# A gated product over 8192 rows: each group's store split into even and odd partitions on two queues, and the second half worked in three pieces

## The chip, the cores and the metric

The kernel runs on one core of one Trainium2 chip. The metric is device time in microseconds of one execution; the time before is the median of three runs. The profile is one more execution, recorded by the hardware profiler.

## The reference

```python
x = np.random.randn(8192, 8192).astype(np.float32)      # fixed seed

def reference(x):
    a, b = np.split(x, 2, axis=-1)        # each 8192 x 4096
    silu_b = b / (1 + np.exp(-b))
    return a * silu_b                     # 8192 x 4096, float32
```

Each element of the input is read once, 268.44 MB, and each element of the output is written once, 134.22 MB.

## The kernel before

The rows are taken four at a time: one partition holds four rows of the input, 128 KB, in two halves of 64 KB. A group is 128 partitions, so 512 rows, and there are 16 groups. There are three tiles of 128 x 16384 float32 (64 KB in a partition): `pack0` and `pack1`, which take the first half (two rows) of even and odd groups, and `extra`, which takes the second half of every group. The gate is worked in place; the products of both halves are written into the group's `pack`, which then is the complete output of the four rows and is stored from there.

```python
R = 4
W = R * half                                   # 16384
xv = x.tensor.reshape([N // R, R * M]).ap()    # 2048 x 32768
ov = out.tensor.reshape([N // R, W]).ap()      # 2048 x 16384
G = N // (P * R)                               # 16 groups
last = G - 1
packs = [pool.tile([P, W], x.dtype, name=f"pack{s}") for s in range(2)]
extra = pool.tile([P, W], x.dtype, name="extra")
# ... ordered(inst, *after): inst waits only for what is named in after
def load(eng, g, h, *after):
    tile_ = extra if h else packs[g % 2]
    return ordered(
        eng.dma_start(out=tile_, in_=xv[g * P : (g + 1) * P, h * W : (h + 1) * W]), *after
    )

def swiglu(g, h, k0, k1, *after, behind=()):
    rows = (extra if h else packs[g % 2]).rearrange("p (k s c) -> p k s c", k=2, s=2)
    o = packs[g % 2].rearrange("p (h k c) -> p h k c", h=2, k=2)
    b = rows[:, k0:k1, 1, :]
    gate = ordered(nc.scalar.activation(out=b, in_=b, func=_SILU), *after)        # L63
    return ordered(
        nc.vector.tensor_mul(out=o[:, h, k0:k1, :], in0=rows[:, k0:k1, 0, :], in1=b),  # L65
        gate, *behind,
    )

def store(eng, g, c0, c1, *after):
    return ordered(
        eng.dma_start(out=ov[g * P : (g + 1) * P, c0:c1], in_=packs[g % 2][:, c0:c1]), *after
    )

first = {0: load(nc.sync, 0, 0)}
second = {0: load(nc.sync, 0, 1)}
first[1] = load(nc.sync, 1, 0)
for g in range(G):
    prod = swiglu(g, 0, 0, 2, first[g])
    prod = swiglu(g, 1, 0, 1, second[g], behind=[prod])
    prod = swiglu(g, 1, 1, 2, behind=[prod])
    if g < last:
        second[g + 1] = load(nc.sync, g + 1, 1, prod)
    stored = store(nc.sync if g >= last - 1 else nc.scalar, g, 0, W, prod)
    if g + 2 < G:
        first[g + 2] = load(nc.sync, g + 2, 0, stored)
```

So the next load of `extra` waits for the last product of the group, which reads it, and the load of the group after next into the same `pack` waits until the store out of it has landed. The stores of the first 14 groups are issued on ScalarE's queue, those of the last two on SP's, on which all loads are.

Of the kernel before, what the change touches and what calls it, by code (L numbers as in the profile page):

```python
# [1 line left out]

# [4 lines left out]

_SILU = mybir.ActivationFunctionType.Silu


@with_exitstack
def kernel(
    ctx: ExitStack,
    tc: tile.TileContext,
    x: bass.AP,
    out: bass.AP,
):

    nc = tc.nc
    N, M = x.shape
    half = M // 2
    P = nc.NUM_PARTITIONS
    R = 4
    W = R * half

    xv = x.tensor.reshape([N // R, R * M]).ap()
    ov = out.tensor.reshape([N // R, W]).ap()
    G = N // (P * R)
    last = G - 1

    pool = ctx.enter_context(tc.tile_pool(name="sbuf", bufs=1))
    ctx.enter_context(tc.manual_schedule())
    packs = [pool.tile([P, W], x.dtype, name=f"pack{s}") for s in range(2)]
    extra = pool.tile([P, W], x.dtype, name="extra")

    ops = []

    def ordered(inst, *after):

        before = [t for t in reversed(ops) if t.ins.engine == inst.ins.engine][:1]
        for t in ops:
            if not any(t is k for k in [*after, *before]):
                tc.declare_no_dep(inst.ins, t.ins, reason="ordered by the other waits")
        ops.append(inst)
        return inst  # L50
# [4 lines that stand above are left out]
            eng.dma_start(out=tile_, in_=xv[g * P : (g + 1) * P, h * W : (h + 1) * W]), *after  # L55
        )

    def swiglu(g, h, k0, k1, *after, behind=()):

        rows = (extra if h else packs[g % 2]).rearrange("p (k s c) -> p k s c", k=2, s=2)  # L60
        o = packs[g % 2].rearrange("p (h k c) -> p h k c", h=2, k=2)
        b = rows[:, k0:k1, 1, :]
        gate = ordered(nc.scalar.activation(out=b, in_=b, func=_SILU), *after)  # L63
        return ordered(
            nc.vector.tensor_mul(out=o[:, h, k0:k1, :], in0=rows[:, k0:k1, 0, :], in1=b),  # L65
            gate, *behind,
        )

    def store(eng, g, c0, c1, *after):
        return ordered(  # L70
            eng.dma_start(out=ov[g * P : (g + 1) * P, c0:c1], in_=packs[g % 2][:, c0:c1]), *after
        )

    first = {0: load(nc.sync, 0, 0)}
    second = {0: load(nc.sync, 0, 1)}
    first[1] = load(nc.sync, 1, 0)
    for g in range(G):
        prod = swiglu(g, 0, 0, 2, first[g])
        prod = swiglu(g, 1, 0, 1, second[g], behind=[prod])
        prod = swiglu(g, 1, 1, 2, behind=[prod])  # L80
        if g < last:
            second[g + 1] = load(nc.sync, g + 1, 1, prod)
        stored = store(nc.sync if g >= last - 1 else nc.scalar, g, 0, W, prod)
        if g + 2 < G:
            first[g + 2] = load(nc.sync, g + 2, 0, stored)


# [1 line left out]
_INS = ['x']  # L89
_OUTS = [((8192, 4096), 'float32')]  # L90


# [23 lines left out]
```

## Time and profile before

| what | value |
| --- | --- |
| time, median of 3 | 967.15 us (965.48 to 969.77) |
| span of the profiled execution | 964.3 us |
| bytes read, written | 268.44 MB, 134.22 MB |
| queue 1 (SP): packets, MB | 4896, 285.21 |
| queue 10 (ScalarE): packets, MB | 2016, 117.44 |
| gate of 128 x 8192, of 128 x 4096 | 7029 ns, 3608 ns |
| product of 128 x 8192, of 128 x 4096 | 8692 ns, 4421 ns |
| issue to landing, median: load of pack, load of extra, store | 29.7, 47.2, 44.2 us |

How to read it: the busy row of the profile cuts the span into 40 equal slices and gives each a digit, the busy share in tenths. The DMA row is the mean over the core's 16 DMA engines. The chain is the work that ended last, followed back from the end; a DMA in it is counted from its issue to its landing, time in the queue included. In the table of stretches the columns are the stretch, its length, the busy time (and instructions) of VectorE, ScalarE and GpSimd, the granted TensorE clock, the DMA share and the GB/s. DVE is VectorE, ACT is ScalarE, POOL is GpSimd, and a name with q behind it is that engine's queue of DMA-issuing instructions.

### The profile page before, as it was taken

The page shows a single profiled execution, that of the slowest core. Times are in us where ns is not written, and L with a number is a line of the kernel's source. Part 1 is how long each engine was busy: PE and PEld are TensorE (multiplying, and loading weights), DVE is VectorE, ACT ScalarE, POOL GpSimd, SP SyncE. Part 2 cuts the span into 40 slices and gives each one's busy share as a digit, 9 for nine tenths or more (in the row PEclk, how much of TensorE's full clock was granted, in tenths as well). Part 3 has the DMA queues.
Part 4 walks back from the last instruction along what each step waited for, and adds up shares of the span by engine and source line. Part 5 has one row for each costly group of instructions (what it writes and reads, how often), then busy time and mean ns, then how long its engine had stood idle before and what let it go on. Part 6 is the DMA issues. An engine that isn't in the chain of part 4 may idle for free.

```text
span 964.3 us, 220 instructions
## 1 busy us (share of the span) xinstructions
DVE 279.2 (29%) x48; ACT 227.7 (24%) x49; POOL 0.2 (0%) x4
## 2 busy tenths in 40 slices
DVE  0423332133321333213332033321333213332250
ACT  1420222202222022220222112222022220222220
POOL 0000000000000000000000000000000000000000
DMA  9999999999999999999999999999999999999998
GB/s 400 427 435 435 413 430 421 421 432 397 435 427 402 435 394 435 424 402 435 413 435 413 391 435 400 435 427 391 435 410 430 410 405 435 392 435 416 432 410 351
DMA packets 6914, 402.67 MB, mean 418 GB/s; under 512 B 768, under 2 KB 768, under 8 KB 768
## 3 DMA queue, kind: packets, MB, share of 16 engines
q1 hardware_dynamic: 4896, 285.21, 71.0%
q10 hardware_dynamic: 2016, 117.44, 28.1%
q14 instruction: 2, 0.02, 0.0%
HBM read 268.44 MB, written 134.22 MB: 418 GB/s over the span
## 4 chain that ended last, share of the span: by engine, by line
DMA 76%; DVE 14%; ACT 6%; DVEq 0%; issue 0%; SPq 0%
DMA extra<-in_x_dram 76%; DVE pack L65 14%; ACT extra L63 6%; DVEq L111 0%; SPq L55 0%
## 5 line engine op out<-in xcount | busy, mean ns | idle before, releaser
L65 DVE TENSOR_TENSOR pack<-pack 128x8192 f32<-128x8192 f32 x16 | 139.1, 8692 | 340.8 <-ACT pack L63 340.8
L65 DVE TENSOR_TENSOR pack<-extra 128x4096 f32<-128x4096 f32 x32 | 140.2, 4421 | 317.2 <-ACT extra L63 317.2
L63 ACT ACTIVATE extra<-extra 128x4096 f32<-128x4096 f32 x32 | 114.0, 3608 | 398.4 <-DMA extra<-in_x_dram 398.4
L63 ACT ACTIVATE pack<-pack 128x8192 f32<-128x8192 f32 x16 | 112.5, 7029 | 305.1 <-DMA pack<-in_x_dram 305.1
L63 ACT ACT_TABLE_LOAD x1 | 1.3, 1283 | 0.7 <-PEq L100 0.7
L100 POOL MEMSET const-bfloat16-1.0<- 128x1 bf16 x1 | 0.1, 101 | 0.0
L100 POOL MEMSET const-uint8-127<- 128x1 uint8 x1 | 0.1, 101 | 0.0
L100 POOL MEMSET const-float32-0.0<- 128x1 f32 x1 | 0.1, 98 | 0.2 <-issue 0.2
L100 POOL MEMSET const-float32-1.0<- 128x1 f32 x1 | 0.1, 98 | 0.0
## 6 DMA issues: line engine op xcount, KB each, us to landing
pack<-in_x_dram SPq DMA_DIRECT2D x16, 29.7
extra<-in_x_dram SPq DMA_DIRECT2D x16, 47.2
out_dram<-pack ACTq DMA_DIRECT2D x14, 44.2
out_dram<-pack SPq DMA_DIRECT2D x2, 37.6
```

The source lines that it names most:

```text
L63: gate = ordered(nc.scalar.activation(out=b, in_=b, func=_SILU), *after)
L65: nc.vector.tensor_mul(out=o[:, h, k0:k1, :], in0=rows[:, k0:k1, 0, :], in1=b),
L100: nc = _bacc.Bacc("TRN2", target_bir_lowering=False, num_devices=1)
```

## The change

Three things are done. The store of each of the first 14 groups becomes two: the 64 even partitions on ScalarE's queue and the 64 odd ones on GpSimd's, so that both can be at work at once; the next load into the `pack` waits for both. The gates and products of the second half are done in three pieces (half a row, half a row, a row) in place of two, so that the first product can start earlier. The last two stores stay whole on SP's queue. The diff, cut to its core:

```diff
-    def swiglu(g, h, k0, k1, *after, behind=()):
-        ... gate of rows k0 to k1, then their product
+    def gate(g, h, k0, k1, c0, c1, *after):
+        b = rows(g, h)[:, k0:k1, 1, c0:c1]
+        return ordered(nc.scalar.activation(out=b, in_=b, func=_SILU), *after)
+    def product(g, h, k0, k1, c0, c1, *after):
+        ... the product of the same columns
-    def store(eng, g, c0, c1, *after):
+    def store(eng, g, parts, *after):
         return ordered(
-            eng.dma_start(out=ov[g * P : (g + 1) * P, c0:c1], in_=packs[g % 2][:, c0:c1]), *after
+            eng.dma_start(out=ov[g * P : (g + 1) * P][parts], in_=packs[g % 2][parts]), *after
         )
+    even, odd, whole = slice(0, P, 2), slice(1, P, 2), slice(0, P)
     ...
     for g in range(G):
-        prod = swiglu(g, 0, 0, 2, first[g])
-        prod = swiglu(g, 1, 0, 1, second[g], behind=[prod])
-        prod = swiglu(g, 1, 1, 2, behind=[prod])
+        prod = product(g, 0, 0, 2, 0, half, gate(g, 0, 0, 2, 0, half, first[g]))
+        pieces = [(0, 0, half // 2), (0, half // 2, half), (1, 0, half)]
+        gated = [gate(g, 1, k, k + 1, c0, c1, second[g]) for k, c0, c1 in pieces]
+        for (k, c0, c1), b in zip(pieces, gated):
+            prod = product(g, 1, k, k + 1, c0, c1, b, prod)
         if g < last:
             second[g + 1] = load(nc.sync, g + 1, 1, prod)
-        stored = store(nc.sync if g >= last - 1 else nc.scalar, g, 0, W, prod)
+        if g < last - 1:
+            stored = [store(nc.scalar, g, even, prod), store(nc.gpsimd, g, odd, prod)]
+        else:
+            stored = [store(nc.sync, g, whole, prod)]
         if g + 2 < G:
-            first[g + 2] = load(nc.sync, g + 2, 0, stored)
+            first[g + 2] = load(nc.sync, g + 2, 0, *stored)
```

More of the change, by code (lines that the diff above doesn't have):

```diff
@@ L56, in load, with rows @@
         )
-    def swiglu(g, h, k0, k1, *after, behind=()):
-        rows = (extra if h else packs[g % 2]).rearrange("p (k s c) -> p k s c", k=2, s=2)
+    def gate(g, h, k0, k1, c0, c1, *after):
+        b = rows(g, h)[:, k0:k1, 1, c0:c1]
+        return ordered(nc.scalar.activation(out=b, in_=b, func=_SILU), *after)
+    def product(g, h, k0, k1, c0, c1, *after):
         o = packs[g % 2].rearrange("p (h k c) -> p h k c", h=2, k=2)
-        b = rows[:, k0:k1, 1, :]
-        gate = ordered(nc.scalar.activation(out=b, in_=b, func=_SILU), *after)
         return ordered(
-            nc.vector.tensor_mul(out=o[:, h, k0:k1, :], in0=rows[:, k0:k1, 0, :], in1=b),
-            gate, *behind,
-        )
-    def store(eng, g, c0, c1, *after):
+            nc.vector.tensor_mul(
+                out=o[:, h, k0:k1, c0:c1],
+                in0=rows(g, h)[:, k0:k1, 0, c0:c1],
+                in1=rows(g, h)[:, k0:k1, 1, c0:c1],
+            ),
+            *after,
+        )
+    def rows(g, h):
+        return (extra if h else packs[g % 2]).rearrange("p (k s c) -> p k s c", k=2, s=2)
+    def store(eng, g, parts, *after):
         return ordered(
-            eng.dma_start(out=ov[g * P : (g + 1) * P, c0:c1], in_=packs[g % 2][:, c0:c1]), *after
+            eng.dma_start(out=ov[g * P : (g + 1) * P][parts], in_=packs[g % 2][parts]), *after
         )
+    even, odd, whole = slice(0, P, 2), slice(1, P, 2), slice(0, P)
     first = {0: load(nc.sync, 0, 0)}
```

## The prediction

> **What bounds the kernel now.** I read the head of the profile first, then the DMA queues, the chain that ended last, the waits of the DMA-issuing queue, and a table of stretches over one group. The head of the page:
>
> ```profile
> span 964.3 us, 220 instructions
> DVE 279.2 (29%) x48; ACT 227.7 (24%) x49; POOL 0.2 (0%) x4
> ...
> DMA  9999999999999999999999999999999999999998
> DMA packets 6914, 402.67 MB, mean 418 GB/s; under 512 B 768, under 2 KB 768, under 8 KB 768
> ```
>
> VectorE and ScalarE are busy under a third of the span; the 16 DMA engines are over 90% busy in every slice but the last. So bytes set the time: 402.67 MB in 964.3 us. The packet records of the trace say what the floor is. There are 6,144 data packets of 65,536 bytes, 384 on each of 16 engines, and an undisturbed one takes 2.418 us. 384 x 2.418 = 928.5 us. About 36 us of the span (3.7%) is therefore loss, and no change that moves the same bytes can gain more than that.
>
> Where the 36 us lies, from the same records: packets longer than 2.42 us add 26.1 us per engine; engines without a packet add 9.6 us (2.0 before the first packet, 2.5 in the last ten us, 5.1 between); 1.2 us follow the last packet; some 1.3 us of overlapping records come off again.
>
> All the slow packets are on queue 1, which carries the loads; every one of the 1,792 store packets on queue 10 took 2.418 us. When are they slow? The stretches of one group, 172.5 being the moment when its predecessor's store is issued and 217 that when this store has landed:
>
> ```profile
> 160.00:172.50 12.50, 8.74 (x2) 7.12 (x2) 0.00 (x0) 1.00 0.98 419
> 172.50:182.50 10.00, 0.02 (x1) 0.00 (x0) 0.00 (x0) 1.00 0.92 334
> 182.50:217.00 34.50, 8.69 (x1) 7.03 (x1) 0.00 (x0) 1.00 1.03 445
> 217.00:222.00 5.00, 0.00 (x0) 0.68 (x1) 0.00 (x0) 1.00 0.92 328
> 222.00:232.50 10.50, 7.53 (x2) 6.45 (x2) 0.00 (x0) 1.00 0.99 418
> ```
>
> The last column is GB/s (a stretch's edge can cut a 1 MB lump, so single values are rough). Two dips stand out. I call them A, after the load of `extra` and the store are issued together, and B, after the store has landed and the next load of `pack` is issued. Summing the packets' excess in the 7 us after each issue: A costs 0.5 to 1.6 us, 1.17 on average over 14; B costs 0.03 to 1.1 us, 0.58 over 14; the first loads 0.64 once. 16.4 + 8.2 + 0.6 = 25.2 of the 26.1 us. In the one A where both transfers are issued on SP (at 895 us) the excess is 0.01 us: there no second queue starts up.
>
> The chain repeats one group sixteen times, and the waits of SP's queue say which step is held by what:
>
> ```profile
> 172.53 0.02 issue
> 172.54 48.76 DMA extra<-in_x_dram
> 221.30 0.02 issue
> 221.32 3.62 ACT extra L63
> 224.95 0.02 issue
> 224.97 8.77 DVE pack L65 x2
> ```
>
> ```profile
> SPq L55 <- DMA out_dram<-pack: 615.5, 14, 45.4
> SPq L55 <- DVE pack L65: 266.6, 15, 52.4
> ```
>
> The chain looks like load, gate, product, load; but during the 12.4 us of gate and products the DMA engines still run at 419 GB/s on the already queued load of `pack`. The 48.76 us for `extra` is queueing: by my packet count 3 packets of `pack`, 8 of `extra` and 8 of the store stand before each engine at A, 19 x 2.418 = 45.9 us plus the dips. The second wait shows that the load of `pack` is held by the store's landing, 44.2 us after its issue in the median; `extra` then has only some 1.3 packets per engine left, so the queue is nearly dry at B. The 5.1 us of missing packets between start and end lie mostly there.
>
> [...] in the middle stretch queue 1 and queue 10 alternate one 2.418 us packet each. [...] Which engine takes which of 64 strided rows no run here shows yet. [...] GpSimd issues no transfer in the kernel before.
>
> **The change part by part.**
> 1. *Two stores per group for g = 0 to 13, on ScalarE's and GpSimd's queues.* Bytes and 64 KB packets are the same; 14 transfers of 4 MB are added by GpSimd. With three queues at work, stores get two of three turns instead of one of two. Before: the first store packet comes 4.5 us after the issue, then 8 pairs x 2 x 2.418 = 38.7 us, together 43.2, against 44.2 measured. After: 4 packets in each store queue, 4 x 3 x 2.418 = 29.0 us, + 4.5 = 33.5[...]: about 34.5 us, 10 us earlier. The next load of `pack` is issued 10 us earlier too, with 4 to 7 packets of `extra` still queued instead of 1.3. That cannot move the floor; it removes the near-dry queue at B. Gain: most of the 5.1 us of gaps, say 4; and B's slow packets only if they come from the drained queue. I take 0.4 us per B instead of 0.58: 14 x 0.18 = 2.5 us.
> 2. *A now starts two queues.* Loss at A was tied to a second queue's start. If the two starts overlap it stays 1.17 us; if they add up it is 2.3. I take 1.5: 14 x 0.33 = 4.6 us lost.
> 3. *Gates and products of the second half in three pieces.* From the rows by form, a gate of 4,096 took 3,608 ns and of 8,192 7,029: 0.835 ns each and 187 ns fixed, so 2,048 take 1,897. Products: 4,421 and 8,692 give 1.043 each and 150 fixed, so 2,286. Gates end at 1.90, 3.79 and 7.40 us; products 1.90 to 4.19, to 6.48, and the third, which waits for the third gate, 7.40 to 11.82. Against 12.43 before (3.62 + 8.77 + two hand-overs): 0.6 us sooner per group, 9 us over 15 if it were on the path. It isn't: eight packets per engine (19 us) of `pack` are queued when `extra` lands, so the engines have work either way. Worth 0.
> 4. *Last two stores on SP*: as before, whole, so nothing moves. In the tail the last store is issued at 937.3 us while earlier packets still run, and the products' 0.6 us there is hidden as well.
>
> Sum: 964.3 - 4 - 2.5 + 4.6 = 962.4 us span. The timed runs are 2.85 us above the span (967.15 against 964.3): 965. [...] I shade it to 963.
>
> **The rivals.**
> - [...] For it: the profile only shows 128-row transfers. [...] I give a marked collision about one in eight.
> - *GpSimd's queue is slow*: [...] it lands last, the load of `pack` is issued when `extra` is gone, and the engines run dry at B. A dry spell of 2 us per group is 28 us: 995. For it: the load waits for both stores, so the slower one counts. Against: there are 10 us of slack before it hurts.
> - *Dips at A add up*, 14 x 1.17 more without a gain at B: 964.3 + 16.4 + 2.85 = 984. *B's slow packets vanish altogether and A stays*: 964.3 - 8.2 - 4.5 + 2.85 = 954. Both within 2%.
> - *The three pieces were on the path*: 9 us less, 956. The stretch at 419 GB/s during gate and products speaks against it.
>
> **Range and chances.** The ceiling of the gain is the 25 us of dips and 5 of gaps, so 2% (under 947.8) would need two thirds of both to go: 6%. The additive case ends at 984, inside 2%; only a collision or a slow GpSimd queue goes beyond 986.5: together 17%. 8 in 10: 950 to 986.
>
> **What would show it.** Store packets of 2.418 us on both store queues: no collision. To landing, some 34 us for both stores and some 40 for the loads of `pack`, up from 29.7. The waits of SP's load queue for the stores down from 615 to about 470 us. GB/s after the issue at A about as before, at B a shallower dip. VectorE busy with 16 more products at 150 ns fixed each, 279.2 + 2.4 = 281.6 us. A mean under 410 GB/s, store packets above 2.5 us, or slices below 9 in the DMA row would make the prediction wrong, as would a dip at A that disappears.

## The result, and the profile after

The changed kernel takes 952.52 us (median of four runs, 949.83 to 955.89), against 966.32 us for the kernel before (median of four). The ratio is 0.9856, with a 95% interval of 0.9812 to 0.9901: 1.4% faster, where I had predicted 0.4%. The prediction's range holds it and so does the likeliest of the three chances (within 2%); the size of the gain was mis-estimated by a factor of three. The ratios here and below are estimates with their own intervals, so they can differ a little from the quotient of the two medians. Two slow executions of the kernel with the pieces alone, of 971.6 and 971.7 us, are not in its ratio.

The head of the page of the changed kernel, with its DMA queues and DMA issues; the last number of an issue row is the median time from issue to landing:

```profile
span 951.1 us, 289 instructions
DVE 281.8 (30%) x64; ACT 229.2 (24%) x65; POOL 7.9 (1%) x18
...
DMA  9999999999999999999999999999999999999997
DMA packets 7138, 402.67 MB, mean 423 GB/s; under 512 B 992, under 2 KB 992, under 8 KB 992
...
q1 hardware_dynamic: 4896, 285.21, 70.6%
q0 software_dynamic: 1120, 58.72, 14.6%
q10 hardware_dynamic: 1120, 58.72, 14.3%
...
pack<-in_x_dram SPq DMA_DIRECT2D x16, 40.1
...
out_dram<-pack ACTq DMA_DIRECT2D x14, 36.9
out_dram<-pack POOLq DMA_DIRECT2D x14, 36.8
```

The bytes are the same and the DMA engines carry them at 423 GB/s instead of 418; the DMA row is 9 in every slice but the last, as before. The stores' bytes are now half on queue 0 (GpSimd) and half on queue 10. Both land in 37 us, 7 us sooner than the one store before; the loads of `pack`, issued sooner, take 40.1 us instead of 29.7, because they stand in the queue longer (issued 10.5 us before `extra` lands, 3.0 before the change).

The waits of SP's queue (engine and line, what it waited for, us in total, times, longest):

```profile
SPq L56 <- DMA out_dram<-pack: 506.2, 14, 37.6
SPq L56 <- DVE pack L66: 363.2, 15, 51.5
```

The wait for the stores fell from 615.5 to 506.2 us over 14 groups, 7.8 us for each. The wait for the product grew by nearly as much: SP is free sooner and waits for the next thing. What matters is where in the queue the load then stands. The stretches of one group, cut at the same events as those shown in the prediction: before A, 10 us after A (173.6), the middle, 5 us after B (211.5), and the rest:

```profile
161.90:173.60 11.70, 8.92 (x3) 7.18 (x3) 0.00 (x0) 1.00 1.03 448
173.60:183.60 10.00, 0.00 (x0) 0.00 (x0) 0.54 (x1) 1.00 0.98 419
183.60:211.50 27.90, 8.69 (x1) 7.03 (x1) 0.00 (x0) 1.00 0.99 418
211.50:216.50 5.00, 0.00 (x0) 0.00 (x0) 0.00 (x0) 1.00 1.12 485
216.50:221.50 5.00, 0.00 (x0) 0.00 (x0) 0.00 (x0) 1.00 1.00 433
```

The dip after B (328 GB/s before) is gone; 485 is above what 16 undisturbed packets of 65,536 bytes in 2.418 us come to (434 GB/s) and shows again that a stretch's edge can cut a 1 MB lump. The dip right after A (334 before) is shallow, but the middle, 445 before, is now 418. So A's loss may have moved rather than gone. The packet records settle it. Sums over the span in us per engine, from the excess of each packet over 2.42 us and from the time in which an engine had no packet:

| term | before | after | difference |
| --- | --- | --- | --- |
| floor, 384 packets x 2.418 us | 928.5 | 928.5 | 0 |
| slow packets of the first loads | 0.6 | 0.6 | 0.0 |
| slow packets within 25 us after A | 16.9 | 15.7 | -1.2 |
| slow packets later, around B | 8.6 | 0.2 | -8.4 |
| engines without a packet, between start and end | 5.1 | 0.5 | -4.6 |
| engines without a packet in the last ten us | 2.5 | 3.5 | +1.0 |

The differences add up to -13.2 us, and the span fell by 13.2. Nearly all of it is B: its slow packets and its gaps. Of A's 15.7 us only 3.1 lie within 5 us of the issue (16.1 before); the rest lies 5 to 25 us after it, when the second store queue has come in too (its first packet starts 6.6 us after the issue in the median, that of queue 10 after 4.2).

The same records show the turns. While the 128 packets of a group's stores went out, the loads started 98 packets before and 50 after, medians over 14 groups; the stores' packets took 36.6 us from first to last before and 30.0 after.

The chain of one group shows the three pieces; start, length, what:

```profile
161.84 0.02 issue
161.87 7.22 ACT extra L61 x3
169.09 0.02 issue
169.11 4.44 DVE pack L66
173.55 0.02 issue
173.57 47.98 DMA extra<-in_x_dram
```

From the landing of `extra` to the next load it is 11.7 us instead of 12.4: three gates, 7.22 us, and the third product. The load after it takes 47.98 us, about as before (48.76).

### The profile page after: what moved, and what is told of

Same layout as the page of the kernel before. It is cut to its first block, busy times and chain, and to the rows that moved or that the text cites. A ratio compares the mean times of both kernels' runs of the same rounds, so it can differ in the third digit from the quotient of the medians.

```text
span 951.1 us, 289 instructions
## 1 busy us (share of the span) xinstructions
DVE 281.8 (30%) x64; ACT 229.2 (24%) x65; POOL 7.9 (1%) x18
## 4 chain that ended last, share of the span: by engine, by line
DMA 77%; ACT 12%; DVE 7%; ACTq 0%; issue 0%; SPq 0%
DMA extra<-in_x_dram 77%; ACT extra L61 12%; DVE pack L66 7%; ACTq L125 0%; SPq L56 0%
## 5 line engine op out<-in xcount | busy, mean ns | idle before, releaser
L66 DVE TENSOR_TENSOR pack<-extra 128x2048 f32<-128x2048 f32 (+1 forms) x48 | 142.7, 3001 | 250.5 <-ACT extra L61 250.5
L61 ACT ACTIVATE extra<-extra 128x2048 f32<-128x2048 f32 (+1 forms) x48 | 115.4, 2467 | 346.0 <-DMA extra<-in_x_dram 346.0
L79 POOL DMA_DIRECT2D out_dram<-pack x14 | 7.7, 548 | 817.4 <-DVE pack L66 817.4
## 6 DMA issues: line engine op xcount, KB each, us to landing
pack<-in_x_dram SPq DMA_DIRECT2D x16, 40.1
out_dram<-pack ACTq DMA_DIRECT2D x14, 36.9
out_dram<-pack POOLq DMA_DIRECT2D x14, 36.8
```

Source lines behind the costliest of these rows:

```text
L61: return ordered(nc.scalar.activation(out=b, in_=b, func=_SILU), *after)
L66: nc.vector.tensor_mul(out=o[:, h, k0:k1, c0:c1], in0=rows(g, h)[:, k0:k1, 0, c0:c1], in1=rows(g, h)[:, k0:k1, 1, c0:c1],),
L79: eng.dma_start(out=ov[g * P : (g + 1) * P][parts], in_=packs[g % 2][parts]), *after
```

## The experiments

The theory after the result: with two store queues the stores take about two of three turns (128 of 178 packets while they go out, against 128 of 226 before), land 7 us sooner, and the next load of `pack` is queued while about 10 us of `extra` is still to come (10.5 us, against 3.0 before), so that SP's queue no longer runs nearly dry at B. The rivals: the three pieces; smaller or gentler stores as such; GpSimd's queue.

**The pieces alone.** The changed kernel with one whole store on ScalarE's queue:

```diff
-            stored = [store(nc.scalar, g, even, prod), store(nc.gpsimd, g, odd, prod)]
+            stored = [store(nc.scalar, g, whole, prod)]
```

> Three pieces in the second half, store whole on ScalarE's queue as in the kernel before. Share theory (two store queues take two of three turns, the store lands 7 us sooner, the next load is queued before the load queue runs dry): no gain from the pieces, 0.998 to 1.002 of before, about 966 us; dips at A (some 1.2 us each) and B (0.6 us each) as before. Rival, the pieces are on the path (0.6 us per group): 957 us, 0.990.

Measured: 963.62 us, ratio 0.9948 (0.9921 to 0.9975). A gain of half a per cent is inside neither expectation. In the profiled run the span is 964.1 us, no shorter than before.

**The split alone.** The changed kernel with two pieces as before:

```diff
-        pieces = [(0, 0, half // 2), (0, half // 2, half), (1, 0, half)]
+        pieces = [(0, 0, half), (1, 0, half)]
```

> Even and odd stores on two queues, the second half in two pieces as before. Share theory: the whole gain stays, 952 to 955 us, 0.986 to 0.989 of before. Rival, the pieces are on the path: 961 us or more, 0.995.

Measured: 949.56 us, ratio 0.9788 (0.9712 to 0.9864). All the gain is there without the pieces. The two runs point to opposite signs for the pieces: alone they seem to gain, and the split seems better without them. So the changed kernel and the split alone were measured again, side by side:

> The changed kernel once more, to be set against the split without the three pieces on the same chip: 950 to 955 us, 0.983 to 0.988 of before.

> The split with two pieces once more. If the pieces are worth nothing, as the share theory has it: within 0.3% of the changed kernel in this call, 950 to 955 us. If the first measurement (949.6 us) was no chance, the three pieces cost something: 3 us less than the changed kernel here too. If the run with the pieces alone (0.995) was no chance, they gain: 3 us or more above it.

Measured: 951.58 us with the pieces, 0.9836 (0.9807 to 0.9865), and 950.18 without, 0.9835 (0.9796 to 0.9873). Beside the split the pieces are worth nothing that can be measured. That they help a little with a single store queue (0.9948) isn't ruled out: there SP waits for the stores as long as before (616.1 us, against 615.5), and the 0.7 us of the shorter chain may count, by my estimate. It stays open: the run with the whole store on GpSimd's queue, below, has the pieces and a single store queue too, and its gain isn't clear of zero.

**Two stores in one queue.**

```diff
-            stored = [store(nc.scalar, g, even, prod), store(nc.gpsimd, g, odd, prod)]
+            stored = [store(nc.scalar, g, even, prod), store(nc.scalar, g, odd, prod)]
```

> Even and odd stores, both on ScalarE's queue, three pieces. Share theory: stores get one of two turns again, last landing 43 to 45 us after the issue, dips at B and the gaps between packets (5 us) are back: 962 to 967 us, 0.996 to 1.001. Rival, the smaller transfer of 64 rows starts more gently (dip at A): the dip at A is gone here too and the time is 954 to 957 us, 0.988 to 0.991.

Measured: 1005.88 us, ratio 1.0384 (1.032 to 1.0448). The gain needs the second queue, as the theory had it, but the 39 us of loss were not foreseen. The rival falls too: 64 rows do not start more gently, as the slow packets in the 7 us after A cost 1.25 us per group, against 1.16 before. The page's DMA issues for these stores:

```profile
out_dram<-pack ACTq DMA_DIRECT2D x28, 36.3
```

The 36.3 us is the median over first and second stores together. The packet records of one group show the rest: after the last packet of the even store queue 10 misses one turn, and 5 to 12 us after the odd store's first packet the packets of both queues are slow once more (1.1 to 1.4 us in 13 of the 14 groups, 0.5 in one). The next load of `pack` is issued 49.5 us after A in the median, 2.3 us before `extra` lands, and the engines are without a packet for 25.2 us over the span instead of 5.1. Cutting a store in two within one queue costs 39 us here; the gain comes with the second queue.

**The whole store on GpSimd's queue.**

```diff
-            stored = [store(nc.scalar, g, even, prod), store(nc.gpsimd, g, odd, prod)]
+            stored = [store(nc.gpsimd, g, whole, prod)]
```

> Whole store of 128 rows on GpSimd's queue alone, none on ScalarE's (but the last two on SP), three pieces. Share theory: one of two turns, landing 44 us or more, about before: 962 to 970 us. Rival, GpSimd's queue starts without disturbing loads, and that is what took the dip at A away: the dip at A is gone, that at B stays, 948 to 956 us.

Measured: 965.45 us, ratio 0.9995 (0.9971 to 1.002). GpSimd's queue as such changes nothing: landing after 44.4 us, store packets of 2.418 us in the mean, slow packets of 16.5 us after A and 7.4 around B, as before. That rival falls, and with it my fear of a slow queue.

**The store held back.** A whole store on ScalarE's queue, after an in-place copy on VectorE that leaves the values as they are; the load of `extra` is issued as before:

```diff
+            held = packs[g % 2][:, 0 : W // 2]
+            held = ordered(nc.vector.tensor_copy(out=held, in_=held), prod)
-            stored = [store(nc.scalar, g, even, prod), store(nc.gpsimd, g, odd, prod)]
+            stored = [store(nc.scalar, g, whole, prod, held)]
```

> Whole store on ScalarE's queue, held back by an in-place copy of 128 x 8192 on VectorE (4 to 9 us) behind the last product; the load of extra is issued as before. Theory, the dip at A belongs to the start of a store in an empty queue [...]: the slow packets move with the store, to 1 to 5 us after its own issue, and none follow the load's issue; still some 1.2 us per group. Rival, the dip belongs to the issue of the load (or to two issues at once): slow packets stay within 5 us of the load's issue, or vanish as the issues are apart. The time is 975 to 1000 us either way, because the store lands later and the next load comes later still.

Measured: 1041.85 us in a single execution, so without an interval, and far above what was expected. The timeline of one group (start, length, engine):

```profile
253.28 4.42 DVE L96 COPY pack<-pack 128x8192 f32<-128x8192 f32 x1
253.39 0.33 SPq L56 DMA_DIRECT2D extra<-in_x_dram  x1
257.73 0.34 ACTq L79 DMA_DIRECT2D out_dram<-pack  x1
```

The load and the store are 4.3 us apart. In this group the loads' packets lose 0.01 us in the 5 us after the load's issue, and 1.08 us in the three after that, which are the first three after the store's issue; over all 14 groups it is at most 0.05 and then 0.5 to 1.4. The dip at A belongs to the start of the store, not to the issue of the load. What the held store costs is a different matter: the next load of `pack` comes 52.9 us after A, 1.1 us before `extra` lands, and the engines are without a packet for 46.8 us. In every other group the packets of both queues are also slow between 10 and 45 us after A (4.0 to 4.8 us per group). Why, no run here shows.

**The load held back.** The changed kernel with both its stores, but the load of `pack` waits for one more gate on data that is then overwritten, of 7.03, 9.59 or 12.15 us. It adds work to ScalarE, which has the time free (busy 24% of the span in the changed kernel):

```diff
+        if 0 < g < last:
+            spare = packs[(g + 1) % 2][:, 0 : W // 2]          # then 0 : 11264, 0 : 14336
+            spare = ordered(nc.scalar.activation(out=spare, in_=spare, func=_SILU), *stored)
+            first[g + 1] = load(nc.sync, g + 1, 0, *stored, spare)
         pieces = ...
-        if g + 2 < G:
-            first[g + 2] = load(nc.sync, g + 2, 0, *stored)
```

> The changed kernel with the next load of pack held back by one more gate of 128 x 8192 on ScalarE (7.03 us, on data that is then overwritten), so that it is issued some 45 us after A instead of 38, where the kernel before has it (44.4). Theory, the load queue that has almost run dry makes the dip at B and the gaps: both come back, 0.6 and 0.3 us per group, and the time is 962 to 968 us. Rival, the gain comes from two store queues as such (shorter stores, gentler start): 951 to 955 us as in the changed kernel.

> As the run with the load of pack held, but by a gate of 128 x 11264 (0.835 ns x 11264 + 187 ns = 9.6 us), so that it is issued some 44 us after A and 5 us before extra lands; held by 7 us it came 7 us before and the time was 956 us. Theory (the nearer the load queue is to dry, the more of the dip at B and of the gaps comes back): 958 to 964 us, 0.991 to 0.997 of before. Rival (two store queues as such): no more than the 956 us.

> The same with 128 x 14336 (12.2 us), issued 2 us before extra lands, later than in the kernel before (2.6 to 4.3 us). Theory: all of the gain is given back and more, 965 to 980 us, with gaps of a us or more per group at B. Rival: 956 us, or a step of at most 2 us.

Measured: 955.96, 962.64 and 979.38 us; ratios 0.9881 (0.9837 to 0.9924), 0.9948 (0.993 to 0.9967), 1.0121 (1.0093 to 1.015). The first delay was too small to tell the theories apart: 955.96 us is inside neither range, its interval overlaps that of the changed kernel, and the load was issued 41.7 us after A and not at the 45 intended, still 6 us before `extra` landed. The other two decide. From the traces, medians and sums in us:

| kernel | B after A | ahead of `extra`'s landing | slow packets around B | gaps between start and end | span |
| --- | --- | --- | --- | --- | --- |
| changed | 37.1 | 10.5 | 0.2 | 0.5 | 951.1 |
| held 7 us | 41.7 | 6.1 | 3.5 | 5.9 | 955.9 |
| held 9.6 us | 44.8 | 3.9 | 5.7 | 5.5 | 960.2 |
| before | 44.2 | 3.0 | 8.6 | 5.1 | 964.3 |
| held 12.2 us | 47.1 | 2.2 | 9.4 | 15.7 | 978.6 |

Two store queues are at work in every row but that of before, and the span follows the third column through all five. With the load issued 44.8 us after A, against 44.2 before, the changed kernel has lost about two thirds of its gain (0.9948, against 0.9856 and 0.9836). What is left may belong to the 0.9 us by which the load is still further ahead of `extra`, or to the pieces; no run separates these. The added gate doesn't hold up other work itself: in all three kernels it ends before `extra` lands, by 0.8 us at the least, and ScalarE's next gate waits for that landing. The waits of SP's queue in the last of these kernels show the held load:

```profile
SPq L56 <- DMA out_dram<-pack: 481.7, 14, 35.5
SPq L56 <- DVE pack L66: 245.2, 15, 51.6
SPq L56 <- ACT pack L90: 170.2, 14, 12.2
```

The stores still land early (34.4 us per wait on average, 36.2 in the changed kernel); 12.2 us per group for the added gate come on top.

**Halves instead of even and odd.**

```diff
-    even, odd, whole = slice(0, P, 2), slice(1, P, 2), slice(0, P)
+    even, odd, whole = slice(0, P // 2), slice(P // 2, P), slice(0, P)
```

> Partitions 0 to 63 on ScalarE's queue, 64 to 127 on GpSimd's, instead of even and odd. [...] 980 to 1150 us. [...] store packets of 2.42 us and 950 to 955 us as in the changed kernel.

Measured: 1046.1 us, ratio 1.0824 (1.076 to 1.0887), 10% above the changed kernel. Its DMA queues and issues:

```profile
DMA packets 7138, 402.67 MB, mean 385 GB/s; under 512 B 992, under 2 KB 992, under 8 KB 992
...
q0 software_dynamic: 1120, 58.72, 16.1%
q10 hardware_dynamic: 1120, 58.72, 13.7%
...
out_dram<-pack ACTq DMA_DIRECT2D x14, 44.2
out_dram<-pack POOLq DMA_DIRECT2D x14, 44.1
```

Packets, bytes and queues are those of the changed kernel; the rate is 385 GB/s and the stores land 7 us later. The share of queue 0 is larger than that of queue 10 for the same bytes, since its packets take 2,995 ns in the mean (6% of them over 4.5 us), against 2,561 on queue 10 and 2,418 undisturbed. Most store packets still take 2.418 us. The two ranges that were expected, for store packets that are slowed and for packets that are not, were my estimates; the time lies in the first. The store packets are not all of the loss either: of the 94 us by which this span is longer than that of the changed kernel they make 37, slower load packets 28, and moments without a packet 29. In the changed kernel the packets on queue 10 never exceed 2,421 ns and 11% of those on queue 0 are over 2.6 us: whatever slows those, the even and odd rows lose far less. What slows the packets of the halves, no run here shows.

**All sixteen groups split.** The split alone, with the last two stores on the two queues as well:

```diff
-        if g < last - 1:
+        if g <= last:
             stored = [store(nc.scalar, g, even, prod), store(nc.gpsimd, g, odd, prod)]
```

> Even and odd stores on the two queues for all 16 groups, two pieces in the second half; nothing but the last two stores differs from the run with the split alone. Theory: in the last two groups no load waits for a store, so an early landing is worth nothing there: 948 to 953 us, no difference. Rival: the last store runs beside a store in SP's queue and ends sooner when it has queues of its own: 945 us or less.

Measured: 967.91 us, ratio 0.9998 (0.9971 to 1.0025). Both expectations missed: the last two stores alone give all of the gain back. The end of it in stretches, with the DMA share and the GB/s last: the second last store, the rest of the load of `extra`, the last gates and products, the last store:

```profile
886.00:921.00 35.00, 9.02 (x2) 7.03 (x1) 0.54 (x1) 1.00 1.01 423
921.00:933.00 12.00, 0.00 (x0) 0.09 (x1) 0.00 (x0) 1.00 0.64 279
933.00:945.00 12.00, 8.44 (x2) 7.04 (x2) 0.00 (x0) 1.00 0.00 0
945.00:967.00 22.00, 0.32 (x1) 0.00 (x0) 0.54 (x1) 1.00 0.88 381
```

The second last store takes its turns at once and is done before the last load has landed (at 932.9 us); then there is nothing to move for the 12 us of the last gates and products (0 GB/s in that stretch; no packet at all from 932.6 to 946.5 us, the start of the last store included). With that store behind the load in SP's queue, as in the changed kernel and before, the load lands first and the store fills these 12 us at 437 GB/s:

```profile
884.00:911.00 27.00, 9.05 (x2) 7.03 (x1) 0.00 (x0) 1.00 0.99 420
911.00:923.00 12.00, 8.63 (x3) 7.22 (x3) 0.00 (x0) 1.00 1.01 437
```

## Why the prediction was right, and where it was off

**The bound and the floor** held: 928.5 us of packets, and a change that can only win back part of the 36 us of loss. That is why the range held, though with little room: 952.5 us lies 2.5 us above its lower end, as both of the larger errors below went the same way.

**Step 1, the earlier landing**, had the right mechanism. The stores got 128 of 178 turns, a little more than the two of three that I had put, an estimate from the alternation of the two queues in the kernel before. The gaps: 4 us predicted, 4.6 measured. B's slow packets are the term that was mis-sized: I allowed 2.5 us of 8.2, because I didn't know whether they came from the drained queue. They do: 8.4 us went, and the runs with the held load bring them back the nearer the queue comes to dry (3.5, 5.7 and 9.4 us, with the load 6.1, 3.9 and 2.2 us ahead). The landing was put at 34.5 us and took 36.8, as the last packets end at 34 us and the landing follows some 3 us later, a term I had left out; 1 us of the 34.5 was an allowance for GpSimd's queue that no trace of the kernel before showed. For the kernel before, my sum of 43.2 us came close to the measured 44.2 only because it counts one turn of 2.4 us too many: the first store packet starts 5.0 us after the issue in the median, the last ends at 41.5, and the landing follows 2.7 us later. So an earlier landing by 10 us was forecast and one by 7 measured; the waits for the stores came to 506 us instead of about 470. The 40 us for the loads of `pack` came out at 40.1.

**Step 2, two starts at A**, was off in sign: 4.6 us lost was predicted, 1.2 us gained was measured. The start of a store is what costs in the run with the held store (0.5 to 1.4 us per group), but the two starts of the changed kernel cost together no more than one whole store does. Why, the runs don't show. I had also written that a dip at A that disappears would speak against me. Right after the issue it nearly did, from 334 to 419 GB/s in the group shown; the loss stands later, between 5 and 25 us. The second store queue alone doesn't explain that move: with the load of `pack` held back by 7.0, 9.6 and 12.2 us, and both store queues at work, 7.7, 11.6 and 17.6 us of slow packets lie within 5 us of A again. The sum at A was wrong, and its mechanism stays open.

**Step 3, the pieces**, was worth nothing, as predicted, and VectorE's 281.8 us against the 281.6 worked out agrees with the 150 ns of fixed cost per product, read from the two sizes in the kernel before. **Step 4** was right that nothing moves; what the arrangement is worth, some 18 us between the run with all groups split (967.9) and that with the split alone (949.6, and 950.2 in the repetition), I had not seen.

**The sum**: a span of 962.4 us was worked out and 951.1 measured. Of the 11.3 us, B accounts for 5.9 (8.4 instead of 2.5), A for 5.8 (1.2 gained instead of 4.6 lost), the gaps for 0.6, and the end, which I hadn't in the sum, took back 1.0. The 2 us by which I shaded the time downwards, for a gentler start of half the rows, were a guess and went in the right direction by luck: in the run with both stores in one queue half the rows start no more gently (1.25 us of slow packets per group after A, against 1.16).

**The rivals**: no marked collision, and no slow GpSimd queue (36.8 us to landing, as on ScalarE's, 36.9). The collision, store packets slowed in stores of 64 rows, was my estimate; no trace of the kernel before showed one. One sign that I had named against me did show: store packets above 2.5 us, on queue 0 (11% over 2.6 us, 3.7 at the most), though its mean is 2.474 us and all slow packets of that queue together come to 3.1 us. With partitions 0 to 63 and 64 to 127 the store packets are slow indeed (2,995 and 2,561 ns in the mean) and the kernel takes 10% longer than the changed one, so the rival deserved the room it got. "B's slow packets vanish altogether and A stays", put at 954 us, is what happened.

## What to carry to other kernels

When DMA engines look always busy, sum the packets' excess over the undisturbed packet and place it in time: the dips and near-dry moments are what could still be won here, 13 of 36 us. In this kernel a second queue for a transfer that others wait for bought it more turns (128 of 178 packets instead of 128 of 226), which paid as its landing released the next load 10.5 us before `extra` landed instead of 3.0; splitting it within one queue, or into partitions 0 to 63 and 64 to 127, lost 4% and 8% here. At the end of this kernel the opposite order pays, some 18 us: let the last load pass first and keep a store to fill the last computation.

## What the runs showed of the hardware that was not expected

- Two stores of 64 rows in one queue were worse than one of 128: a missed turn between them, and a second dip of 1.1 to 1.4 us in nearly every group (1005.9 us, against 963.6 with the whole store and the same pieces).
- A store on ScalarE's queue took longer to issue with 64 rows than with 128: 479 ns for the even rows and 473 for partitions 0 to 63, against 362 ns. On GpSimd's it made next to no difference: 539 ns for the odd rows, 533 for all 128.
- In the run with the store held back, its packets and those of the loads were both slow in the middle of the store, in every other group, 4.0 to 4.8 us each time. The cause stays open.
